# Recurrent mixer: block-diagonal matrices kept as 64 columns, products on the halves of the array

## The chip, the cores and the metric

The kernel runs on one core of a Trainium2 chip. TensorE multiplies, VectorE, ScalarE and GpSimd do the elementwise work, SyncE issues most DMAs. The metric is the device time of one execution in microseconds; smaller is better. Before the change three runs took 2711.81, 2712.51 and 2715.53 us, median 2712.51.

## The reference

The whole kernel computes two transformer-like blocks on 256 tokens: two layers with windowed attention and retention, then a layer with a recurrent mixer beside a latent attention, a layer with two more attentions, and a mixture of experts. The change touches one piece, the recurrent mixer (RWKV-7), with 8 heads of 64 features:

```python
def step(state, inp):
    r_t, w_t, k_t, v_t, kk_t, b_t = inp
    sa = jnp.einsum('bhvk,bhk->bhv', state, -kk_t)
    state = (state * w_t[:, :, None, :] + sa[..., None] * b_t[:, :, None, :]
             + v_t[..., None] * k_t[:, :, None, :])
    return state, jnp.einsum('bhvk,bhk->bhv', state, r_t)

_, y = lax.scan(step, state0, xs)        # 256 steps
```

It is followed by a group norm, a bonus term and a gate. All of it is fp32.

## The kernel before

The 256 steps are done in four chunks of 64. Inside a chunk the recurrence becomes matrix algebra: products between the chunk's keys and removal vectors, masked to a triangle, the inverse of a unit triangular 64x64 matrix, and a few products with the state. Only the state passes from chunk to chunk. Two chunks lie on the 128 partitions at once (a token tile `tt` of 128), so such a matrix is stored as 128x128 with two 64x64 blocks on the diagonal and zeros elsewhere, four heads side by side in a tile of 128x512 (`X`, line 153). The helper `each` (line 165) multiplies four of them into one PSUM tile with four matmuls of 128 columns.

The heads come in two groups `g` of four. `blocks` (line 226) makes the 16x16 diagonal blocks of the triangular matrices of all heads: four sets of four products (L163), masked on VectorE (L243), reduced to 16 columns (L245), written to memory (L247) and read back in another layout (L249). `inverses` (line 254) inverts all the 16x16 blocks at once on VectorE (L266, L268), through memory again (L271, L274). `group` (line 305) is a generator that runs once for each group: it extends the inverse to 64x64 (x, xt, p1 and the products b1, b2, L336 to L359), makes the factors tmt, wz, abr and akr, and then loops over the two chunks of the token tile: u from wz, the state and tmt (L384, L385), the new state (L392, L393) and the output (L397 to L399).

Head pairs share 128 partitions (head 2j on the lower 64, head 2j+1 on the upper), so k, r and wz of a single head are kept in zero-padded tiles zk, zr, zw and contracted over all 128 rows. Values and u get the same treatment for the chunks: vz and uz have one tile for each chunk with zeros in the other half, set once by GpSimd (L302).

What sets the order: the two `group` generators and the latent attention `mla` are advanced in turn by `rounds` (line 1335), and the tile framework's scheduler then orders each engine's queue from what is recorded. On TensorE the `blocks` products stand between the last input projections (L518 to L520, in fp32r, three passes for a high and a low part), and the last chunks between the first matmuls of the output projection.

In the trace a line of the form `sm<-zk,a 128*128 128x128 f32` is a matmul into tile sm: 128 rows times 128 columns of weights, and the moving operand of 128 rows and 128 columns. Every fp32 matmul shows up as two instructions. The tiles bb, kd, kb and kn of the code appear as a, kn, em (their buffers' names), wz as zw, and b1, b2, p1 as b and p.

Of the kernel before, what the change touches and what calls it, by code (L numbers as in the profile page):

```python
# [44 lines left out]
def _const_parts():  # L45
    f = np.float32
    i128 = np.arange(P)
    out = {}
# [6 lines left out]
    t = np.arange(S)  # L55
# [37 lines left out]
    s_ = i128[:, None]  # L93
    t_ = i128[None, :]
# [4 lines left out]
    out["m16"] = (b16 & up).astype(f)
    out["m1"] = (b32 & ~b16 & up).astype(f)  # L100
    out["m2"] = (b64 & ~b32 & up).astype(f)
    out["minc"] = (b64 & (s_ <= t_)).astype(f)
    out["mlow"] = (b64 & (s_ > t_)).astype(f)
    out["mb16"] = b16.astype(f)
# [38 lines left out]
class Rwkv:  # L143
# [18 lines left out]
    def mm(self, o, l, r):  # L162
        self.nc.tensor.matmul(o, l, r, start=True, stop=True)  # L163

    def each(self, fn):
        ps = self.b.smps()
        for i in range(4):
            fn(ps[:, i * P:i * P + P], i)
        return ps.rearrange("p (h t) -> p h t", h=4)

    def decays(self):

# [52 lines left out]
    def blocks(self):  # L225

        nc, b, mp = self.nc, self.b, self.mp
        self.z = []
        for g in range(2):
            z = [self.X(f"z{n}{g}") for n in "krw"]  # L230
            for t in z:
                for par in range(2):
                    nc.gpsimd.memset(t[64 - 64 * par:P - 64 * par, par::2], 0.0)
            self.z.append(z)
        lc = b.mk(mp, [P, 16, 16], F32, "b20")
        for tt in range(2):
            ts = slice(tt * P, tt * P + P)
            for g in range(2):
                zk = self.z[g][0]
                self.padded(zk, self.kd, g, ts)  # L240
                ps = self.each(lambda o, i: self.mm(o, self.bb[:, 2 * g + i // 2, ts], zk[:, i]))
                t = b.t2k().rearrange("p (h t) -> p h t", h=4)
                nc.vector.tensor_tensor(t, ps, self.mask("m16"), op=OP.mult)  # L243
                s0 = 8 * tt + 4 * g
                nc.vector.tensor_reduce(lc[:, s0:s0 + 4], t.rearrange("p h (b j) -> p h j b", b=8), axis=AX.X, op=OP.add)  # L245
        d1 = b.mk(b.dp, [16, P, 16], F32, "d1")
        nc.sync.dma_start(out=d1.rearrange("h s j -> s h j"), in_=lc)  # L247
        self.nt = b.mk(mp, [P, 16, 16], F32, "x0")
        nc.sync.dma_start(out=self.nt, in_=d1.rearrange("h (b i) j -> (h b) i j", i=16))  # L249

    def mask(self, m):
        return self.b.c(m)[:, None, :].to_broadcast([P, 4, P])

    def inverses(self):

# [20 lines left out]
    def queries(self):  # L276
# [21 lines left out]
        self.vz = [[b.mk(self.mp, [P, S], F32, f"vz{c}{g}") for c in range(2)] for g in range(2)]  # L298
        for g in range(2):
            for c in range(2):  # L300
                for t in (self.uz[g][c], self.vz[g][c]):
                    nc.gpsimd.memset(t[64 - 64 * c:P - 64 * c], 0.0)  # L302

    def group(self, g, yt):

# [5 lines left out]
        uz, vz = self.uz[g], self.vz[g]  # L311
        sg_ = self.st[:, 2 * g:2 * g + 2]
        X = lambda tag: self.X(tag + str(g))
        mb = b.c("mb16").rearrange("p (b j) -> p b j", b=8)[:, None].to_broadcast([P, 4, 8, 16])
        pr = lambda i: 2 * g + i // 2
        f = lambda i: slice(64 * i, 64 * i + 64)
        oj = lambda ps, i: ps[64 * (i % 2):64 * (i % 2) + 64, (i // 2) * 64:(i // 2) * 64 + 64]
        for tt in range(2):
            ts = slice(tt * P, tt * P + P)
            self.padded(zk, kd, g, ts)  # L320
            self.padded(zr, r, g, ts)

            tk = {}
            for n, src in (("kkt", kd), ("bbt", bb), ("kbt", kb), ("v", v)):
                ps = b.smps()
                for i in range(2):
                    nc.tensor.transpose(ps[:, i * P:i * P + P], src[:, 2 * g + i, ts], b.c("ident"))
                if n == "v":
                    for c in range(2):
                        nc.scalar.copy(vz[c][64 * c:64 * c + 64], ps[64 * c:64 * c + 64, :S])  # L330
                else:
                    tk[n] = b.mk(mp, [P, S], F32, n + str(g))
                    nc.scalar.copy(tk[n], ps[:, :S])
            b1, b2, p1 = X("b1"), X("b2"), X("p1")
            ps = each(lambda o, i: mm(o, bb[:, pr(i), ts], zk[:, i]))
            TT(b1, ps, self.mask("m1"), op=OP.mult)  # L336
            TT(b2, ps, self.mask("m2"), op=OP.mult)

            x, xt = X("x"), X("xt")
            s0 = 8 * tt + 4 * g  # L340
            for m, dst in ((0, x), (1, xt)):
                nc.gpsimd.tensor_tensor(dst.rearrange("p h (b j) -> p h b j", b=8),
                                        self.xc[:, m, s0:s0 + 4, None, :].to_broadcast([P, 4, 8, 16]), mb, op=OP.mult)
            yield
            nc.scalar.copy(p1, each(lambda o, i: mm(o, b1[:, i], x[:, i])))
            yield
            q1 = each(lambda o, i: mm(o, xt[:, i], p1[:, i]))
            TT(x, x, q1, op=OP.subtract)
            yield
            q2 = each(lambda o, i: mm(o, p1[:, i], xt[:, i]))  # L350
            TT(xt, xt, q2, op=OP.subtract)
            yield
            nc.scalar.copy(p1, each(lambda o, i: mm(o, b2[:, i], x[:, i])))
            ml = X("b1")
            ps = each(lambda o, i: mm(o, zk[:, i], kb[:, pr(i), ts]))
            TT(ml, ps, self.mask("mlow"), op=OP.mult)
            yield
            q2 = each(lambda o, i: mm(o, p1[:, i], xt[:, i]))
            TT(xt, xt, q2, op=OP.subtract)  # L359
            abr, akr = X("abr"), X("akr")  # L360
            ps = each(lambda o, i: mm(o, bb[:, pr(i), ts], zr[:, i]))
            TT(abr, ps, self.mask("minc"), op=OP.mult)
            yield
            tmt = X("tmt")
            nc.scalar.activation(tmt, each(lambda o, i: mm(o, ml[:, i], xt[:, i])), AF.Copy, scale=-1.0)
            ps = b.smps()
            for i in range(4):
                par = i % 2
                mm(ps[64 * par:64 * par + 64, (i // 2) * P:(i // 2) * P + P], tk["kkt"][:, f(i)], xt[:, i])
            for par in range(2):  # L370
                rows = slice(64 * par, 64 * par + 64)
                nc.scalar.activation(wz[rows, par::2], ps[rows, :S].rearrange("p (j t) -> p j t", j=2), AF.Copy, scale=-1.0)
            yield
            ps = each(lambda o, i: mm(o, kb[:, pr(i), ts], zr[:, i]))
            TT(akr, ps, self.mask("minc"), op=OP.mult)
            yield

            for c in range(2):
# [1627 lines left out]
```

## Time and profile before

| What | Value |
|---|---|
| median of three runs | 2712.51 us |
| the profiled execution's own time | 2711.97 us |
| its span, first to last instruction | 2710.2 us |
| TensorE busy | 2657.4 us, 98% of the span |
| VectorE / ScalarE / GpSimd busy | 73% / 58% / 7% |
| mean granted TensorE clock | 0.993 |
| matmul instructions | 15024 |

The span is what the trace covers; the execution's own time is 1.8 us longer. The busy share is an average over stages that differ much: the mixer's part is the roughly 120 us from 1188 to 1309 us, and it is read by itself below. The granted clock is 1 when TensorE runs at 2.4 GHz and 0.5 at 1.2 GHz.

### The profile page before, as it was taken

How to read it: one execution, taken by the hardware profiler on the slowest of the kernel's cores; microseconds unless marked ns; L12 is line 12 of the kernel's file. 1: busy time of each engine (PE TensorE's matmuls, PEld its weight loads, DVE VectorE, ACT ScalarE, POOL GpSimd, SP SyncE). 2: the span in 40 equal slices, each digit the busy share in tenths (PEclk: the TensorE clock that was granted, in tenths of full speed). 3: DMA queues.
4: the chain of work that ended last, by engine and by line, in shares of the span. 5: the costliest groups of instructions: out<-in, count | busy, mean ns of one | idle time of the engine just before them, and what ended most of it. 6: DMA issues, size and time to landing. Idle time of an engine off the chain costs nothing.

```text
span 2710.2 us, 39506 instructions
## 1 busy us (share of the span) xinstructions
PE 2657.4 (98%) x15024; PEld 2201.5 (81%) x15024; DVE 1975.8 (73%) x2951; ACT 1567.9 (58%) x2364; POOL 197.2 (7%) x244
## 2 busy tenths in 40 slices
PE   7999999999999999999999999999999999999998
PEld 5866788888887899888899988888887787788776
DVE  5255577767765687675655568999988898888886
ACT  4244444144355666564454465877777777777775
POOL 1121200000113100312200100000000000000000
PEclk9999999999999999999999999999999999999999
DMA  7244223444542265530355455999899999998992
GB/s 289 73 167 149 74 101 131 153 140 162 181 133 78 95 209 176 168 125 6 109 183 193 166 182 192 359 356 370 329 355 350 357 333 361 347 358 332 364 349 91
DMA packets 113875, 585.94 MB, mean 216 GB/s; under 512 B 19536, under 2 KB 23136, under 8 KB 68752
## 3 DMA queue, kind: packets, MB, share of 16 engines
q1 hardware_dynamic: 111440, 576.19, 58.8%
q0 software_dynamic: 2240, 7.16, 1.1%
q8 instruction: 120, 1.97, 0.3%
q14 instruction: 75, 0.61, 0.1%
HBM read 581.82 MB, written 1.47 MB: 215 GB/s over the span
## 4 chain that ended last, share of the span: by engine, by line
PE 63%; DVE 2%; ACT 1%; DMA 1%; issue 1%; POOL 0%; DVEq 0%; POOLq 0%; ACTq 0%
PE mm L519 14%; PE mm L518 14%; PE mm L520 14%; PE dn L519 4%; PE dn L518 4%; PE dn L520 4%; PE sm L163 1%; PE sm L1785 1%; DVE wl L488 1%; PE sm L589 1%; PE sm L1735 1%; ACT wh L487 0%; PE sm L574 0%; PE sm L1223 0%; DMA wf<-w_in 0%
## 5 line engine op out<-in xcount | busy, mean ns | idle before, releaser
L488 DVE TENSOR_TENSOR wl<-wf,wh 128x1024 fp32r<-128x1024 f32 (+3 forms) x1178 | 1215.0, 1060 | 362.3 <-ACT wh L487 356.6
L487 ACT CAST wh<-wf 128x1024 fp32r<-128x1024 f32 (+3 forms) x1178 | 1044.1, 912 | 564.1 <-PE mm L519 282.5
L518 PE MATMUL mm<-ah,wh 128*128 128x256 f32 (+1 forms) x1768 | 569.6, 325 | 3.8 <-ACT wh L487 1.7
L520 PE MATMUL mm<-ah,wl 128*128 128x256 f32 (+1 forms) x1768 | 567.4, 322 | 0.9 <-DVE wl L488 0.7
L519 PE MATMUL mm<-al,wh 128*128 128x256 f32 (+1 forms) x1768 | 567.6, 322 | 0.0
L518 PEld LDWEIGHTS mm<-ah,wh 128*128 128x128 f32 x1768 | 330.2, 188 | 43.4 <-issue 7.8
L519 PE MATMUL mm<-wl,xh 128*128 128x512 f32 x896 | 357.7, 399 | 2.0 <-DVE wl L488 2.0
L519 PEld LDWEIGHTS mm<-al,wh 128*128 128x128 f32 x1768 | 332.3, 188 | 32.3 <-issue 5.5
L520 PEld LDWEIGHTS mm<-ah,wl 128*128 128x128 f32 x1768 | 333.2, 189 | 30.8 <-issue 2.3
L518 PE MATMUL mm<-wh,xh 128*128 128x512 f32 x896 | 355.2, 396 | 0.0
L520 PE MATMUL mm<-wh,xl 128*128 128x512 f32 x896 | 353.4, 395 | 0.0
L519 PEld LDWEIGHTS mm<-wl,xh 128*128 128x128 f32 x896 | 168.2, 188 | 52.2 <-DVE wl L488 13.1
L518 PEld LDWEIGHTS mm<-wh,xh 128*128 128x128 f32 x896 | 168.3, 188 | 39.4 <-ACT xh L1737 0.2
L520 PEld LDWEIGHTS mm<-wh,xl 128*128 128x128 f32 x896 | 168.2, 188 | 37.3
L520 PE MATMUL dn<-wh,eal 128*128 128x512 f32 x448 | 180.6, 403 | 0.0
L519 PE MATMUL dn<-wl,eah 128*128 128x512 f32 x448 | 177.8, 397 | 0.0
L518 PE MATMUL mm<-gh,wh 128*128 128x256 f32 (+1 forms) x528 | 168.6, 319 | 0.0
L520 PE MATMUL mm<-gh,wl 128*128 128x256 f32 (+1 forms) x528 | 168.0, 318 | 0.0
L519 PE MATMUL mm<-gl,wh 128*128 128x256 f32 (+1 forms) x528 | 168.0, 318 | 0.0
L518 PE MATMUL dn<-wh,eah 128*128 128x512 f32 x448 | 157.7, 396 | 0.0
L520 PEld LDWEIGHTS mm<-gh,wl 128*128 128x128 f32 x528 | 99.9, 189 | 7.9
L519 PEld LDWEIGHTS mm<-gl,wh 128*128 128x128 f32 x528 | 99.9, 189 | 7.7
(514 smaller groups left out, 3426.9 us busy)
## 6 DMA issues: line engine op xcount, KB each, us to landing
wf<-moe_wg SPq DMA_DIRECT2D x112, 1024.0 KB, 6.9
wf<-moe_wu SPq DMA_DIRECT2D x112, 1024.0 KB, 6.8
wf<-moe_wd SPq DMA_DIRECT2D x112, 1024.0 KB, 6.4
wf<-w_mod SPq DMA_DIRECT2D x64, 768.0 KB, 4.4
wf<-w_up SPq DMA_DIRECT2D x88, 512.0 KB, 3.5
wf<-w_down SPq DMA_DIRECT2D x32, 704.0 KB, 4.0
wf<-w_out SPq DMA_DIRECT2D x32, 512.0 KB, 3.5
wf<-w_qkg SPq DMA_DIRECT2D x30, 512.0 KB, 4.6
```

The source lines that it names most:

```text
L163: self.nc.tensor.matmul(o, l, r, start=True, stop=True)
L487: nc.scalar.copy(dh, src)
L488: nc.vector.tensor_tensor(dl, src, dh.bitcast(F32), op=OP.subtract)
L518: nc.tensor.matmul(out, lh, rh, start=first, stop=False)
L519: nc.tensor.matmul(out, lh, rl, start=False, stop=False)
L520: nc.tensor.matmul(out, ll, rh, start=False, stop=last)
L589: self.nc.tensor.matmul(ps[:w.shape[1], :S], w, self.com[:, :S], start=True, stop=True)
L1735: nc.tensor.matmul(ps[:, m * S:m * S + S], src[:, tt, k * P:k * P + P], G[:, tt, e0:e0 + 2], start=tt == 0, stop=tt == 1)
L1785: nc.tensor.transpose(ps[:, j * P:j * P + P], s[:, j * P:j * P + P], self.c("ident"))
```

## The change

`X` tiles get 64 columns for each head instead of 128: partition s holds only its own block's columns. The masks are cut the same way (`own`), so masking, copying and subtracting work on 128x256 instead of 128x512 elements. `each` now makes eight matmuls of 64 columns: for each head one for the lower and one for the upper 64 tokens, which go to the lower and the upper 64 partitions of PSUM. Products of two compact tiles (`blocks`, the new local function) contract over 64 rows: they use 64 rows and 64 columns of the array, the lower or the upper half of each. Products with a zero-padded operand (zk, zr, wz) still contract over 128 rows, now with 64 columns of weights. In the chunk loop the products with u and v read just the 64 rows of their chunk, so v needs no padding: the vz tiles and the memsets go. wz is made for each chunk by itself.

The heart of the diff (the mask constants, reshapes with b=4 for b=8, and the shapes of the x and xt products change in the same way and are left out):

```diff
     def X(self, tag):
-        return self.b.mk(self.mp, [P, 4, P], F32, tag)
+        return self.b.mk(self.mp, [P, 4, 64], F32, tag)
...
     def each(self, fn):
         ps = self.b.smps()
         for i in range(4):
-            fn(ps[:, i * P:i * P + P], i)
-        return ps.rearrange("p (h t) -> p h t", h=4)
+            for c in range(2):
+                self.mm(ps[64 * c:64 * c + 64, 64 * i:64 * i + 64], *fn(i, slice(64 * c, 64 * c + 64)))
+        return ps[:, :S].rearrange("p (h t) -> p h t", h=4)
...
-                ps = self.each(lambda o, i: self.mm(o, self.bb[:, 2 * g + i // 2, ts], zk[:, i]))
+                ps = self.each(lambda i, cs: (self.bb[:, 2 * g + i // 2, ts][:, cs], zk[:, i, cs]))
...
+        blocks = lambda l, r: each(lambda i, cs: (l[cs, i], r[cs, i]))
+            of = lambda t: lambda i, cs: t[:, pr(i), ts][:, cs]
...
-            nc.scalar.copy(p1, each(lambda o, i: mm(o, b1[:, i], x[:, i])))
+            nc.scalar.copy(p1, blocks(b1, x))
...
-            ps = each(lambda o, i: mm(o, zk[:, i], kb[:, pr(i), ts]))
+            ps = each(lambda i, cs: (zk[:, i, cs], of(kb)(i, cs)))
...
-            ps = b.smps()
-            for i in range(4):
-                par = i % 2
-                mm(ps[64 * par:64 * par + 64, (i // 2) * P:(i // 2) * P + P], tk["kkt"][:, f(i)], xt[:, i])
+            for c, ps in enumerate((b.smps(), b.smps())):
+                cs = slice(64 * c, 64 * c + 64)
+                for i in range(4):
+                    mm(oj(ps, i), tk["kkt"][cs, f(i)], xt[cs, i])
...
-                    nc.tensor.matmul(up[cs, f(i)], tmt[:, i, cs], vz[c][:, f(i)], start=ch == 0, stop=True)
+                    nc.tensor.matmul(up[cs, f(i)], tmt[cs, i], vt[cs, f(i)], start=ch == 0, stop=True)
...
-                        nc.tensor.matmul(oj(sp, i), tk["bbt"][:, f(i)], u[:, f(i)], start=True, stop=False)
-                        nc.tensor.matmul(oj(sp, i), tk["kbt"][:, f(i)], vz[c][:, f(i)], start=False, stop=True)
+                        nc.tensor.matmul(oj(sp, i), tk["bbt"][cs, f(i)], u[cs, f(i)], start=True, stop=False)
+                        nc.tensor.matmul(oj(sp, i), tk["kbt"][cs, f(i)], vt[cs, f(i)], start=False, stop=True)
...
-                    nc.tensor.matmul(oj(yp, i), u[:, f(i)], abr[:, i, cs], start=ch == 0, stop=False)
-                    nc.tensor.matmul(oj(yp, i), vz[c][:, f(i)], akr[:, i, cs], start=False, stop=True)
+                    nc.tensor.matmul(oj(yp, i), u[cs, f(i)], abr[cs, i], start=ch == 0, stop=False)
+                    nc.tensor.matmul(oj(yp, i), vt[cs, f(i)], akr[cs, i], start=False, stop=True)
```

Line numbers after the change are one to three lower from line 334 on: L163 becomes L165, L384 and L385 become L383 and L384, L397 to L399 become L396 to L398, L518 to L520 become L517 to L519.

In TensorE's queue the first set of `blocks` stands like this before (sm is the set's PSUM tile, zk and a its operands, the mm rows are an input projection):

```order
L520 MATMUL mm_10803<-ah_10081,wl_10796 128x256
L163 MATMUL sm_10751<-zk_1961_10730,a_10462 128x128
L518 MATMUL mm_10803<-ah_10081,wh_10795 128x256
L163 MATMUL sm_10751<-zk_1961_10730,a_10462 128x128
L519 MATMUL mm_10803<-al_10082,wh_10795 128x256
L163 MATMUL sm_10751<-zk_1961_10730,a_10462 128x128
L520 MATMUL mm_10803<-ah_10081,wl_10796 128x256
L163 MATMUL sm_10751<-zk_1961_10730,a_10462 128x128
L518 MATMUL mm_10803<-ah_10081,wh_10799 128x256
L519 MATMUL mm_10803<-al_10082,wh_10799 128x256
```

and like this after:

```order
L519 MATMUL mm_10819<-ah_10081,wl_10812 128x256
L165 MATMUL sm_10751<-zk_1961_10730,a_10462 64x64
L517 MATMUL mm_10819<-ah_10081,wh_10811 128x256
L165 MATMUL sm_10751<-zk_1961_10730,a_10462 64x64
L518 MATMUL mm_10819<-al_10082,wh_10811 128x256
L165 MATMUL sm_10751<-zk_1961_10730,a_10462 64x64
L519 MATMUL mm_10819<-ah_10081,wl_10812 128x256
L165 MATMUL sm_10751<-zk_1961_10730,a_10462 64x64
L517 MATMUL mm_10819<-ah_10081,wh_10815 128x256
L165 MATMUL sm_10751<-zk_1961_10730,a_10462 64x64
L518 MATMUL mm_10819<-al_10082,wh_10815 128x256
L165 MATMUL sm_10751<-zk_1961_10730,a_10462 64x64
```

Four rows of 128x128 become eight of 64x64, and they still alternate one by one with the projection's full-width rows, so twice as many of those stand between the first and the last product of the set.

In the middle of the first group phase, TensorE's queue before (x, b, p and xt are compact matrices, em, zk and zr operands over all 128 rows; rows of both groups alternate):

```order
L163 MATMUL sm_11253<-x_2039_11091,b_2036_11082 128x128 x4
L163 MATMUL sm_11260<-em_10465,zk_1961_10730 128x128 x4
L163 MATMUL sm_11282<-x_2064_11165,b_2061_11156 128x128 x4
L163 MATMUL sm_11289<-em_10465,zk_1964_10739 128x128 x4
L163 MATMUL sm_11295<-xt_2040_11092,p_2037_11083 128x128 x4
L163 MATMUL sm_11303<-zr_1962_10731,a_10462 128x128 x4
```

and after:

```order
L165 MATMUL sm_11289<-x_2036_11099,b_2033_11086 64x64 x8
L165 MATMUL sm_11300<-em_10465,zk_1961_10730 64x64 x8
L165 MATMUL sm_11326<-x_2062_11177,b_2059_11164 64x64 x8
L165 MATMUL sm_11337<-em_10465,zk_1964_10739 64x64 x8
L165 MATMUL sm_11347<-xt_2037_11100,p_2034_11087 64x64 x8
L165 MATMUL sm_11359<-zr_1962_10731,a_10462 64x64 x8
```

The order of the sets stays, with eight small products for four. What the rows can't show: the sets of b and x and of xt and p now contract over 64 rows, those of em with zk and of zr with a over 128.

VectorE's queue behind the third and fourth set of `blocks`, before (L243 masks, L245 reduces, L488 splits weights, L282 is a product of the next step, `queries`):

```order
L243 TENSOR_TENSOR t2k_10776<-sm_10771,cB_1864_10233 128x512
L243 TENSOR_TENSOR t2k_10786<-sm_10781,cB_1864_10233 128x512
L245 TENSOR_REDUCE b_1967_10748<-t2k_10776 128x64
L245 TENSOR_REDUCE b_1967_10748<-t2k_10786 128x64
L488 TENSOR_TENSOR wl_10946<-wf_10943,wh_10945 128x512
L488 TENSOR_TENSOR wl_10950<-wf_10943,wh_10949 128x512
L1294 SCALAR_TENSOR_TENSOR v_10237<-mm_10840,V_61,v_10237 128x255
L282 TENSOR_TENSOR cum_10463<-r_10235,k_10236 128x1024
```

and after:

```order
L247 TENSOR_TENSOR t2k_10788<-sm_10779,cB_1864_10233 128x256
L487 TENSOR_TENSOR wl_10890<-wf_10883,wh_10889 128x512
L249 TENSOR_REDUCE b_1967_10748<-t2k_10788 128x64
L487 TENSOR_TENSOR wl_10962<-wf_10959,wh_10961 128x512
L247 TENSOR_TENSOR t2k_10802<-sm_10793,cB_1864_10233 128x256
L286 TENSOR_TENSOR cum_10463<-r_10235,k_10236 128x1024
L249 TENSOR_REDUCE b_1967_10748<-t2k_10802 128x64
```

The mask of the last set is no longer directly ahead of its reduction: the 128x1024 product of `queries` (now L286) has moved between them.

## Rows read from the trace of the kernel before

**Rows 1.** The page: engines' busy time, and the last chain by engine.

```profile
PE 2657.4 (98%) x15024; PEld 2201.5 (81%) x15024; DVE 1975.8 (73%) x2951; ACT 1567.9 (58%) x2364; POOL 197.2 (7%) x244
...
PE 63%; DVE 2%; ACT 1%; DMA 1%; issue 1%; POOL 0%; DVEq 0%; POOLq 0%; ACTq 0%
```

**Rows 2.** Table by stretches: length, then busy us of each engine (instructions).

```profile
1187.90:1204.80 16.90, 16.90 (x146) 16.90 (x145) 14.68 (x21) 7.81 (x16) 5.73 (x12) 1.00 0.56 153
1204.80:1218.70 13.90, 10.81 (x62) 8.80 (x60) 12.00 (x46) 8.10 (x22) 2.92 (x6) 0.88 0.27 100
1218.70:1309.10 90.40, 88.84 (x912) 75.63 (x912) 46.88 (x118) 40.30 (x113) 14.85 (x20) 1.00 0.04 8
```

**Rows 3.** The same table for line 163 alone, the third stage.

```profile
1218.70:1309.10 90.40, 40.29 (x336) 37.57 (x336) 1.00 0.04 8
```

**Rows 4.** Waits of TensorE in the third stage: total us, times, longest.

```profile
PE sm L1239 <- DVE t2k L1235: 1.3, 1, 1.3
```

**Rows 5.** Timeline, TensorE, full products: start us, duration us, then the instructions.

```profile
1240.32 1.06 PE L163 MATMUL sm<-zr,a 128*128 128x128 f32 x8
1241.21 1.06 PE L163 MATMUL sm<-xt,b 128*128 128x128 f32 x8
```

**Rows 6.** Timeline, TensorE, narrow products that alternate column halves.

```profile
1250.07 0.33 PE L398 MATMUL sm<-abr,uz 128*64 128x64 f32 x4
...
1250.30 0.34 PE L398 MATMUL sm<-abr,uz 128*64 128x64 f32 x4
```

**Rows 7.** Timeline, TensorE, narrow products on one column half.

```profile
1252.78 0.28 PE L385 MATMUL sm<-vz,tmt 128*64 128x64 f32 x2
1252.90 0.28 PE L384 MATMUL sm<-st,zw 128*64 128x64 f32 x2
```

**Rows 8.** Timeline, TensorE, from narrow to full and back.

```profile
1305.03 0.22 PE L398 MATMUL sm<-abr,uz 128*64 128x64 f32 x1
1305.18 0.39 PE L519 MATMUL mm<-al,wh 128*128 128x256 f32 x1
1305.41 0.28 PE L520 MATMUL mm<-ah,wl 128*128 128x256 f32 x1
1305.62 0.27 PE L399 MATMUL sm<-akr,vz 128*64 128x64 f32 x1
...
1305.72 0.22 PE L399 MATMUL sm<-akr,vz 128*64 128x64 f32 x1
```

**Rows 9.** Timeline, TensorE, `blocks` between the projections.

```profile
1187.57 0.28 PE L518 MATMUL mm<-ah,wh 128*128 128x256 f32 x1
1187.69 0.28 PE L519 MATMUL mm<-al,wh 128*128 128x256 f32 x1
...
1187.93 0.38 PE L163 MATMUL sm<-zk,a 128*128 128x128 f32 x2
...
1188.28 0.38 PE L163 MATMUL sm<-zk,a 128*128 128x128 f32 x2
...
1193.66 0.38 PE L163 MATMUL sm<-zk,a 128*128 128x128 f32 x2
```

**Rows 10.** Chain of waits across the inverses: start us, us, what.

```profile
1198.34 3.83 DMA d<-b
...
1205.01 0.24 DVE xt L266
...
1217.49 0.39 DVE b L269
...
1223.10 1.40 POOL x L342 x2
```

**Rows 11.** Groups by line on VectorE, 1187.5 to 1219 us.

```profile
L245 DVE TENSOR_REDUCE b<-t2k 128x64 f32<-128x512 f32 x4 | 4.1, 1034 | 0.0
...
L282 DVE TENSOR_TENSOR cum<-r,k 128x1024 f32<-128x1024 f32 x1 | 1.2, 1214 | 0.0
...
L1331 DVE TENSOR_TENSOR t2k<-mm,cB 128x256 f32<-128x256 f32 x1 | 0.4, 417 | 0.0
```

More of the change, by code (lines that the diff above doesn't have):

```diff
@@ L98, in _const_parts @@
     up = s_ < t_
[L99 to L104, printed above, removed]
+    own = lambda m: np.where(s_ < 64, m[:, :64], m[:, 64:]).astype(f)
+    out["m16"] = own(b16 & up)
+    out["m1"] = own(b32 & ~b16 & up)
+    out["m2"] = own(b64 & ~b32 & up)
+    out["minc"] = own(b64 & (s_ <= t_))
+    out["mlow"] = own(b64 & (s_ > t_))
+    out["mb16"] = own(b16)
     out["seg"] = np.tile((np.arange(S) % 64 != 0).astype(f), (P, 1))
@@ L229, in blocks @@
         for g in range(2):
-            z = [self.X(f"z{n}{g}") for n in "krw"]
+            z = [self.b.mk(mp, [P, 4, P], F32, f"z{n}{g}") for n in "krw"]
             for t in z:
@@ L240, in blocks @@
                 self.padded(zk, self.kd, g, ts)
-                ps = self.each(lambda o, i: self.mm(o, self.bb[:, 2 * g + i // 2, ts], zk[:, i]))
-                t = b.t2k().rearrange("p (h t) -> p h t", h=4)
+                ps = self.each(lambda i, cs: (self.bb[:, 2 * g + i // 2, ts][:, cs], zk[:, i, cs]))
+                t = b.t2k()[:, :S].rearrange("p (h t) -> p h t", h=4)
                 nc.vector.tensor_tensor(t, ps, self.mask("m16"), op=OP.mult)
                 s0 = 8 * tt + 4 * g
-                nc.vector.tensor_reduce(lc[:, s0:s0 + 4], t.rearrange("p h (b j) -> p h j b", b=8), axis=AX.X, op=OP.add)
+                nc.vector.tensor_reduce(lc[:, s0:s0 + 4], t.rearrange("p h (b j) -> p h j b", b=4), axis=AX.X, op=OP.add)
         d1 = b.mk(b.dp, [16, P, 16], F32, "d1")
@@ L251, in mask @@
     def mask(self, m):
-        return self.b.c(m)[:, None, :].to_broadcast([P, 4, P])
+        return self.b.c(m)[:, None, :].to_broadcast([P, 4, 64])
     def inverses(self):
@@ L297, in queries @@
         self.uz = [[b.mk(self.mp, [P, S], F32, f"uz{c}{g}") for c in range(2)] for g in range(2)]
[L298 to L302, printed above, removed]
     def group(self, g, yt):
@@ L310, in group @@
         zk, zr, wz = self.z[g]
-        uz, vz = self.uz[g], self.vz[g]
+        uz = self.uz[g]
         sg_ = self.st[:, 2 * g:2 * g + 2]
         X = lambda tag: self.X(tag + str(g))
-        mb = b.c("mb16").rearrange("p (b j) -> p b j", b=8)[:, None].to_broadcast([P, 4, 8, 16])
+        mb = b.c("mb16").rearrange("p (b j) -> p b j", b=4)[:, None].to_broadcast([P, 4, 4, 16])
         pr = lambda i: 2 * g + i // 2
@@ L327, in group @@
                     nc.tensor.transpose(ps[:, i * P:i * P + P], src[:, 2 * g + i, ts], b.c("ident"))
[L328 to L333, printed above, removed]
+                tk[n] = b.mk(mp, [P, S], F32, n + str(g))
+                nc.scalar.copy(tk[n], ps[:, :S])
+            vt = tk["v"]
             b1, b2, p1 = X("b1"), X("b2"), X("p1")
-            ps = each(lambda o, i: mm(o, bb[:, pr(i), ts], zk[:, i]))
+            ps = each(lambda i, cs: (of(bb)(i, cs), zk[:, i, cs]))
             TT(b1, ps, self.mask("m1"), op=OP.mult)
@@ L341, in group @@
             for m, dst in ((0, x), (1, xt)):
-                nc.gpsimd.tensor_tensor(dst.rearrange("p h (b j) -> p h b j", b=8),
-                                        self.xc[:, m, s0:s0 + 4, None, :].to_broadcast([P, 4, 8, 16]), mb, op=OP.mult)
+                nc.gpsimd.tensor_tensor(dst.rearrange("p h (b j) -> p h b j", b=4),
+                                        self.xc[:, m, s0:s0 + 4, None, :].to_broadcast([P, 4, 4, 16]), mb, op=OP.mult)
             yield
-            nc.scalar.copy(p1, each(lambda o, i: mm(o, b1[:, i], x[:, i])))
+            nc.scalar.copy(p1, blocks(b1, x))
             yield
-            q1 = each(lambda o, i: mm(o, xt[:, i], p1[:, i]))
+            q1 = blocks(xt, p1)
             TT(x, x, q1, op=OP.subtract)
             yield
-            q2 = each(lambda o, i: mm(o, p1[:, i], xt[:, i]))
+            q2 = blocks(p1, xt)
             TT(xt, xt, q2, op=OP.subtract)
             yield
-            nc.scalar.copy(p1, each(lambda o, i: mm(o, b2[:, i], x[:, i])))
+            nc.scalar.copy(p1, blocks(b2, x))
             ml = X("b1")
-            ps = each(lambda o, i: mm(o, zk[:, i], kb[:, pr(i), ts]))
+            ps = each(lambda i, cs: (zk[:, i, cs], of(kb)(i, cs)))
             TT(ml, ps, self.mask("mlow"), op=OP.mult)
             yield
-            q2 = each(lambda o, i: mm(o, p1[:, i], xt[:, i]))
+            q2 = blocks(p1, xt)
             TT(xt, xt, q2, op=OP.subtract)
             abr, akr = X("abr"), X("akr")
-            ps = each(lambda o, i: mm(o, bb[:, pr(i), ts], zr[:, i]))
+            ps = each(lambda i, cs: (of(bb)(i, cs), zr[:, i, cs]))
             TT(abr, ps, self.mask("minc"), op=OP.mult)
@@ L364, in group @@
             tmt = X("tmt")
-            nc.scalar.activation(tmt, each(lambda o, i: mm(o, ml[:, i], xt[:, i])), AF.Copy, scale=-1.0)
-            ps = b.smps()
-            for i in range(4):
-                par = i % 2
-                mm(ps[64 * par:64 * par + 64, (i // 2) * P:(i // 2) * P + P], tk["kkt"][:, f(i)], xt[:, i])
-            for par in range(2):
-                rows = slice(64 * par, 64 * par + 64)
-                nc.scalar.activation(wz[rows, par::2], ps[rows, :S].rearrange("p (j t) -> p j t", j=2), AF.Copy, scale=-1.0)
+            nc.scalar.activation(tmt, blocks(ml, xt), AF.Copy, scale=-1.0)
+            for c, ps in enumerate((b.smps(), b.smps())):
+                cs = slice(64 * c, 64 * c + 64)
+                for i in range(4):
+                    mm(oj(ps, i), tk["kkt"][cs, f(i)], xt[cs, i])
+                for par in range(2):
+                    rows = slice(64 * par, 64 * par + 64)
+                    nc.scalar.activation(wz[rows, par::2, cs], ps[rows, :P].rearrange("p (j t) -> p j t", j=2), AF.Copy, scale=-1.0)
             yield
-            ps = each(lambda o, i: mm(o, kb[:, pr(i), ts], zr[:, i]))
+            ps = each(lambda i, cs: (of(kb)(i, cs), zr[:, i, cs]))
             TT(akr, ps, self.mask("minc"), op=OP.mult)
```

## The prediction

> **What bounds the kernel now.** I read the page first: TensorE is busy 2657.4 of 2710.2 us and the chain of work that ended last is 63% TensorE matmuls [rows 1]. The change touches only the recurrent mixer, so the next view is the table by stretches, cut where the mixer's phases change [rows 2]. From 1187.9 to 1204.8 us the four sets of products of `blocks` are interleaved with the last input projections, and TensorE is busy 16.90 of 16.90 us. From 1204.8 to 1218.7 it is busy 10.81 of 13.90 us: this stage waits for the small triangular inverses. From 1218.7 to 1309.1 run both `group` generators and the attention between them: 88.84 of 90.40 us busy at a granted clock of 1.00. The view of waits shows how little TensorE waits there: its longest wait is 1.3 us [rows 4]. So in the first and third stage TensorE's own time is the time, and the halved evictions on VectorE, ScalarE and GpSimd can return at most those 1.6 idle us. In the second stage the chain of waits counts [rows 10]: a DMA that starts at 1198.34, the inverses on VectorE from 1205.01 to 1217.88, and two more DMAs until GpSimd builds x at 1223.10. That is 24.8 us which the change leaves alone, except that GpSimd's tiles halve.
>
> **What a product costs in each shape.** Line 163 takes 40.29 us of the third stage [rows 3]. A `matmul` in fp32 shows up as two instructions. A set of four full products (128x128 weights, 128 columns) starts at 1240.32, the next at 1241.21: 0.89 us a set [rows 5]. With 64 weight columns and 64 moving columns a product on one half of the array takes 0.117 us (1252.78 to 1252.90) [rows 7]. When consecutive products alternate between the two column halves they overlap: four products, eight instructions, in 0.23 us (1250.07 to 1250.30), which is 0.058 us each [rows 6]. So a set of eight small products takes 0.47 us if the halves overlap and 0.94 us if they do not. The unchanged 0.89 us lies between the two, nearly at the slower one.
>
> The third price is that of changing the width. At 1305.03 a 64-wide product starts, and the full one behind it at 1305.18 instead of 0.06 us later: 0.09 us lost. The next full one comes 0.23 us on, where 0.12 is the pace (1187.57 to 1187.69 [rows 9]): 0.11 lost. The way back loses 0.09 us (1305.41 to 1305.62) and then 0.05 (1305.62 to 1305.72 instead of 0.058) [rows 8]. Going to the full array costs 0.20 us, to the narrow one 0.14, a round trip 0.34.
>
> **Part 1, `blocks`.** Before, full fp32 products alternate with full fp32r products at 0.34 us a pair (1187.93 to 1188.28), which is 0.22 + 0.12: the alternation is free, because both use the whole array [rows 9]. After the change the order of TensorE's queue has 32 narrow products up to the end of the fourth set, and 36 full ones between them, with 27 round trips. That is 36 x 0.12 + 32 x 0.117 + 27 x 0.34 = 4.3 + 3.7 + 9.2 = 17.2 us from 1187.93, so the fourth set ends near 1205.1; before, its last product starts at 1193.66. VectorE then has the mask (0.42 us at 128x256, as L1331), a 1.21 us product (L282) that the new order puts ahead of the last reduction, and that reduction (half of 1.03) [rows 11]: 2.2 us, so the DMA starts near 1207.3 instead of 1198.34. That is 9 us later. GpSimd's first two tiles, half as long (1.40 us for two in the chain [rows 10]), return 0.6. I take +8 us at the start of the groups. Bounds: 0, if the alternation is free as it was before (the fourth set then ends near 1196, and VectorE, which lagged 4 us behind it, ends where it did), and +9. TensorE's own queue agrees: the stage grows by 9 us, and the 13.9 us behind it, of which 3.1 are idle, cannot hide more than those.
>
> **Part 2, the groups.** From the queue's order between L1439/L1440 and the last chunk: 38 sets fall from 0.89 to 0.47 us, -16.0 us. The four kkt products per set are now eight on quarters of the array, about -0.8. Changes between full and 64 columns go from 47 to 49, +0.3. New are 113 changes between products with 128 rows (the zero-padded zk, zr and wz are still contracted over 128) and products with 64 rows. No row shows one, since every matmul before has 128 rows. Nearest is the change to 64 columns at 0.14 us; 0 and 0.20 are the ends. At 0.14 they cost +15.8 us. 90 of them are inside the chunk loop, where L383 and L384 now alternate, as do L396 and the pair L397, L398. In the three later y blocks of each group the overlap of column halves goes too, since each head changes rows before the other half follows: 24 instructions took 0.70 us at the overlapped pace and take 1.40 alone, six times, +4.2. Sum -16.0 - 0.8 + 0.3 + 15.8 + 4.2 = +3.5; with some idle time at the joints I take +4.
>
> A rule speaks for this price. The Trainium skill, "TensorEngine Tiling (Array Packing)", Key Properties, says that changing the tiling mode, not just the tile, drains the engine. The 0.09 us gaps of [rows 8] agree for the width; that it holds for rows no row here shows. By the rule the sum stands; without it the 15.8 and the 4.2 go.
>
> **Part 3, the rest.** Eight memsets on GpSimd vanish, four copies of v replace eight on ScalarE, eight wz evictions become sixteen shorter ones: all beside TensorE's 88.84 busy us, so nothing, and at worst the 1.6 idle us grow by as much again.
>
> **Sum.** The profiled execution took 2711.97 us, 0.5 under the median of the three, 2712.51. 2711.97 + 8 + 4 = 2724 us. Later stages are bound by TensorE and would carry a shift through.
>
> **Rivals.**
> - *The change of rows is free.* For it: the 128-row and the 64-row product on one column half use the same columns, and only width changes are seen to cost. Against: the array is re-partitioned in both cases. It is one mechanism and lands on the other side of zero: the loop's 20.0 us vanish and the sets' 16.8 stay, so 2711.97 + 8 - 16.5 = 2703.5 us. It decides as soon as a row change costs under about 0.05 us (then 16.5 - 5.7 - half of 4.2 outweighs the 8).
> - *The two row halves do not overlap.* Both halves of a set write one PSUM tile, and the trace has no row halves. The 24 sets between compact tiles then take 0.94 instead of 0.47 us: +11.3, 2735 us. With the chunk loop's s and y products held up too it is more. A page has this as a rule: the Trainium skill, "TensorEngine Tiling (Array Packing)", Gotcha 1, says that different row tiles cannot access the same PSUM bank at once; no row here shows whether that holds when the partitions differ.
> - *The delay of `blocks` is absorbed.* The inverses' chain has VectorE work of other parts between its steps (12.9 us for 31 short instructions), which could move ahead of the wait; then only the 4 of the groups remain: 2716 us. Against: the DMAs before it are serial and their start is what moves.
>
> **How the numbers follow.** Forecast 0.54, free row changes 0.22, no overlap of row halves 0.12, absorbed delay 0.12. About 0.2% (5.4 us) is what a measurement can tell from no change, so "same" is 2707 to 2718. Faster 0.21: nearly all of the first rival. Same 0.18: the absorbed delay and the low end of the forecast, where a row change costs 0.08 or less. Slower 0.61: the rest of the forecast, and the missing overlap. The forecast's own range, a row change between 0.08 and 0.20 us and +5 to +9 for `blocks`, is 2714 to 2732. The range to hold 8 in 10 reaches into the rivals: 2701 (both gains: free rows and a part of the 8 hidden) to 2738 (no overlap).
>
> **What would show it.** Right: L165 in the narrow products of `blocks` with gaps of about 0.15 and 0.21 us around each full product, the DMA d<-b starting near 1207, and the stretch of the groups near 94 us. In the chunk loop L383 to L384 would start about 0.2 us after each other instead of 0.06. Wrong: L383 and L384 at the old pace (first rival); sets L165 between compact tiles at 0.94 us (second); x by GpSimd before 1228 (third). A drop of the granted clock below 1.00 inside the groups would add time that none of these terms holds: it was 1.00 over the whole stage before, narrow products included [rows 2].

## The result, and the profile after

The changed kernel takes 2742.8 us (median of 4 runs, 2739.8 to 2751.0), beside 2712.8 us of four runs of the kernel before: a ratio of 1.0114, 95% interval 1.0101 to 1.0128. The medians are 30 us apart, where 12 were forecast, and the time lies above the range's upper end of 2738. The profiled execution has a span of 2738.0 us at a mean granted clock of 0.985; before it was 2710.2 us at 0.993. Of the experiments' executions one, at 3062 us and a granted clock of 0.803, was disturbed and stands in none of the times below.

The table by stretches, cut where the same phases begin, has the columns of [rows 2]; the number behind the instruction counts is the granted clock. First the kernel before, its third stage cut once more: at GpSimd's first x, at the first chunk loop and at its end.

```profile
1222.90:1248.40 25.50, 25.34 (x204) 22.03 (x200) 14.42 (x33) 11.95 (x30) 12.61 (x15) 1.00 0.04 5
1248.40:1309.10 60.70, 59.33 (x693) 51.01 (x692) 29.58 (x81) 26.79 (x80) 2.23 (x5) 1.00 0.01 2
```

The changed kernel: `blocks`, the wait for the inverses, the first sets, and the chunk loops (with the second half's sets between them).

```profile
1187.90:1212.20 24.30, 24.30 (x166) 19.57 (x166) 10.66 (x18) 7.85 (x16) 6.95 (x13) 1.00 0.35 96
1212.20:1232.30 20.10, 17.40 (x98) 11.83 (x97) 13.54 (x50) 8.26 (x20) 1.58 (x4) 0.75 0.28 79
1232.30:1252.90 20.60, 18.37 (x362) 14.77 (x357) 10.85 (x31) 11.10 (x34) 8.38 (x15) 1.00 0.06 7
1252.90:1340.80 87.90, 85.78 (x870) 65.10 (x868) 27.01 (x82) 25.72 (x83) 1.98 (x5) 0.77 0.01 3
```

GpSimd's timeline has its first x 9.5 us later than the 1223.10 of [rows 10]: the forecast's +8.

```profile
1232.56 1.41 POOL L340 TENSOR_TENSOR x<-xc,cB 128x256 f32<-128x256 f32 x2 [13.74 <-DMA xc<-d]
```

The first sets fall from 25.5 to 20.6 us. The chunk loops grow from 60.7 to 87.9 us, and there the column of the granted clock reads 0.77 instead of 1.00. A clock of 0.77 over 87.9 us is 0.23 x 87.9 = 20.2 us lost; without it the loops would have taken 67.7. That sum takes everything in the slow stretches as doubled, and so it is an upper estimate: row changes slow down less (0.14 to 0.19 us, below), 48 of them stand in the slow stretches of this trace, and 48 x 0.045 makes the loss nearer 18. The sums below go by the 20.2. So of +31.7 us at the end of the groups (1340.8 against 1309.1) 9.4 stand ahead of them, -4.9 in the sets, +7.0 in the loops at full clock, and +20.2 are the clock. At the program's end 27.8 of the 31.7 are left. Forecast were +8, then +4 for sets and loops together, and for the clock nothing.

The same stretch in slices of 8 us shows that the clock goes between its two levels, 2.4 and 1.2 GHz, and that TensorE is fully busy at the lower one:

```profile
1248.00:1256.00 8.00, 7.36 (x152) 6.06 (x150) 4.04 (x15) 5.42 (x20) 1.84 (x3) 1.00 0.01 2
1256.00:1264.00 8.00, 8.00 (x58) 5.48 (x57) 0.29 (x1) 1.11 (x3) 0.00 (x0) 0.57 0.01 2
1264.00:1272.00 8.00, 8.00 (x61) 6.14 (x61) 2.43 (x9) 1.62 (x6) 1.19 (x3) 0.71 0.00 0
1272.00:1280.00 8.00, 8.00 (x50) 6.07 (x49) 1.01 (x3) 1.47 (x5) 0.80 (x2) 0.50 0.01 2
1280.00:1288.00 8.00, 8.00 (x51) 5.17 (x51) 3.27 (x8) 3.08 (x10) 0.00 (x0) 0.72 0.00 0
1288.00:1296.00 8.00, 6.48 (x130) 5.20 (x126) 3.94 (x12) 3.71 (x13) 0.00 (x0) 1.00 0.01 2
...
1304.00:1312.00 8.00, 8.00 (x131) 6.20 (x127) 3.76 (x12) 4.92 (x17) 0.00 (x0) 1.00 0.01 2
...
1320.00:1328.00 8.00, 8.00 (x36) 5.88 (x37) 0.58 (x2) 1.49 (x4) 0.00 (x0) 0.50 0.00 0
```

Read the instruction counts beside the busy time: 36 to 61 instructions fill 8.00 us in the slow slices, 130 to 152 stand in those at 1.00, sets among them. The busy column alone hides both the slower clock and the gaps: in the rows below a product's duration reaches past the start of the next one even where the two are 0.26 or 0.40 us apart. TensorE's waits say the same. In the whole of the two last stretches the longest is this one (total us, times, longest us),

```profile
PE sm L1238 <- DVE t2k L1234: 2.8, 3, 1.5
```

where it was 1.3 before [rows 4]. TensorE's idle time in these two stretches went from 1.5 to 4.4 us, so waits took some 3 us and not the 22.

The timeline of the chunk loop in the changed kernel, first at half clock, then at full clock (start us, duration us, then the instructions; L383 contracts over 128 rows, L384 over 64):

```profile
1257.52 0.42 PE L398 MATMUL sm<-akr,v 64*64 64x64 f32 x2
1257.87 0.47 PE L383 MATMUL sm<-st,zw 128*64 128x64 f32 x2
...
1258.68 0.47 PE L383 MATMUL sm<-st,zw 128*64 128x64 f32 x2
1259.08 0.47 PE L384 MATMUL sm<-v,tmt 64*64 64x64 f32 x2
1259.48 0.47 PE L383 MATMUL sm<-st,zw 128*64 128x64 f32 x2
...
1264.10 0.33 PE L383 MATMUL sm<-st,zw 128*64 128x64 f32 x2
1264.36 0.33 PE L384 MATMUL sm<-v,tmt 64*64 64x64 f32 x2
1264.61 0.33 PE L383 MATMUL sm<-st,zw 128*64 128x64 f32 x2
...
1267.04 0.28 PE L398 MATMUL sm<-akr,v 64*64 64x64 f32 x2
...
1269.76 0.31 PE L397 MATMUL sm<-abr,uz 64*64 64x64 f32 x1
1269.86 0.42 PE L398 MATMUL sm<-akr,v 64*64 64x64 f32 x2
1270.21 2.07 PE L1452 MATMUL mm<-ql,wuqr 128*128 128x256 f32 x4
```

At full clock a product follows the other after 0.26 us, where 0.117 is its pace without a change of rows [rows 7]: 0.14 a change, the forecast's value. At half clock it is 0.40, against 0.21 for two instructions at that clock's pace (0.10 from 1269.76 to 1269.86): 0.19. The last row shows who pays as well: the attention's full products between the loops run at half clock too, four instructions in 2.07 us. Before they took half of that:

```profile
1220.54 1.03 PE L1453 MATMUL mm<-ql,wuqr 128*128 128x256 f32 x4
```

### The profile page after: what moved, and what is told of

It reads as the page before. It is cut to its first block, busy times and chain, and to the rows that moved or that the text cites. A ratio compares the mean times of both kernels' runs of the same rounds, so it can differ in the third digit from the quotient of the medians.

```text
span 2738.0 us, 40265 instructions
## 1 busy us (share of the span) xinstructions
PE 2682.3 (98%) x15408; PEld 2206.7 (81%) x15408; DVE 1964.9 (72%) x2951; ACT 1565.5 (57%) x2368; POOL 191.4 (7%) x236
## 4 chain that ended last, share of the span: by engine, by line
PE 63%; DVE 2%; ACT 1%; issue 1%; DMA 1%; POOL 0%; DVEq 0%; ACTq 0%; POOLq 0%; SPq 0%
PE mm L518 14%; PE mm L517 14%; PE mm L519 14%; PE dn L518 4%; PE dn L517 4%; PE dn L519 4%; PE sm L165 1%; PE sm L1784 1%; PE sm L588 1%; DVE wl L487 1%; PE sm L1734 1%; ACT wh L486 0%; PE sm L1222 0%; PE sm L397 0%; PE sm L384 0%
## 5 line engine op out<-in xcount | busy, mean ns | idle before, releaser
L517 PE MATMUL mm<-ah,wh 128*128 128x256 f32 (+1 forms) x1768 | 569.7, 326 | 3.9 <-ACT wh L486 1.7
L519 PE MATMUL mm<-ah,wl 128*128 128x256 f32 (+1 forms) x1768 | 567.0, 322 | 1.0 <-DVE wl L487 0.7
L518 PE MATMUL mm<-al,wh 128*128 128x256 f32 (+1 forms) x1768 | 567.4, 322 | 0.0
L517 PEld LDWEIGHTS mm<-ah,wh 128*128 128x128 f32 x1768 | 331.3, 188 | 45.0 <-issue 7.8
L518 PE MATMUL mm<-wl,xh 128*128 128x512 f32 x896 | 357.9, 399 | 2.0 <-DVE wl L487 2.0
L518 PEld LDWEIGHTS mm<-al,wh 128*128 128x128 f32 x1768 | 333.1, 188 | 32.8 <-issue 5.5
L519 PEld LDWEIGHTS mm<-ah,wl 128*128 128x128 f32 x1768 | 332.7, 188 | 31.7 <-issue 2.5
L517 PE MATMUL mm<-wh,xh 128*128 128x512 f32 x896 | 354.6, 396 | 0.0
L519 PE MATMUL mm<-wh,xl 128*128 128x512 f32 x896 | 353.7, 395 | 0.0
L518 PEld LDWEIGHTS mm<-wl,xh 128*128 128x128 f32 x896 | 168.2, 188 | 52.4 <-DVE wl L487 13.1
L517 PEld LDWEIGHTS mm<-wh,xh 128*128 128x128 f32 x896 | 168.3, 188 | 39.4 <-ACT xh L1736 0.2
L519 PEld LDWEIGHTS mm<-wh,xl 128*128 128x128 f32 x896 | 168.3, 188 | 37.0
L519 PE MATMUL dn<-wh,eal 128*128 128x512 f32 x448 | 180.6, 403 | 0.0
L518 PE MATMUL dn<-wl,eah 128*128 128x512 f32 x448 | 177.7, 397 | 0.0
L517 PE MATMUL mm<-gh,wh 128*128 128x256 f32 (+1 forms) x528 | 168.6, 319 | 0.0
L519 PE MATMUL mm<-gh,wl 128*128 128x256 f32 (+1 forms) x528 | 168.0, 318 | 0.0
L518 PE MATMUL mm<-gl,wh 128*128 128x256 f32 (+1 forms) x528 | 168.0, 318 | 0.0
L517 PE MATMUL dn<-wh,eah 128*128 128x512 f32 x448 | 157.7, 396 | 0.0
L519 PEld LDWEIGHTS mm<-gh,wl 128*128 128x128 f32 x528 | 99.9, 189 | 7.9
L518 PEld LDWEIGHTS mm<-gl,wh 128*128 128x128 f32 x528 | 99.9, 189 | 7.7
```

Source lines behind the costliest of these rows:

```text
L517: nc.tensor.matmul(out, lh, rh, start=first, stop=False)
L518: nc.tensor.matmul(out, lh, rl, start=False, stop=False)
L519: nc.tensor.matmul(out, ll, rh, start=False, stop=last)
```

## The experiments

Theory A: a change of rows empties the array for 0.14 us, and the chunk loops, which have little else in them, let the granted clock fall to 1.2 GHz. Theory B: quarter-array products do that by themselves, in any order. Theory C: the clock falls because the stage before starts later and waits longer. "Row changes" counts, in the order of TensorE's queue over the whole program, the neighbours of which one has 128 rows and the other 64: 142 in the changed kernel, none before. Ratios are against the kernel before on the same chip: 2713.0 us (median of 23) for the first four experiments, 2713.7 (of 13) for the others. In the code, `nc.tensor.` and most start and stop arguments are left out, and ... stands for further lines of the same kind.

**Chunk loop back at 128 rows.** The tiles stay compact; v and u get their zero halves back.

```
- matmul(up[cs, f(i)], tmt[cs, i], vt[cs, f(i)])
+ matmul(up[cs, f(i)], tmt[:, i], vz[c][:, f(i)])
- matmul(oj(yp, i), u[cs, f(i)], abr[cs, i])
+ matmul(oj(yp, i), u[:, f(i)], abr[:, i])
...
```

> The changed kernel with the chunk loop alone put back to 128 rows (v and u padded with zeros as before); the sets and `blocks` stay compact. Row changes in TensorE's queue fall from 142 to 34 in the whole program. Theory A (each row change empties the array for 0.14 us, and these gaps let the granted clock fall to 1.2 GHz in the chunk loops, which costs some 20 us more): 108 x 0.14 = 15, 4 for the overlap and 20 for the clock come back, near 2743 - 39 = 2704 us, granted clock 1.00 in the loops. Theory B (64-row products lower the clock by themselves, whatever their order): the loops have none left, so 2704 too, but a clock below 1.00 among the compact sets. Theory C (the clock falls because the stage before starts later and has longer gaps): the clock still falls, 2724.

Measured: 2711.2 us, ratio 0.999 (0.9978 to 1.0003), so the whole loss of 30 us is gone. Its chunk loops, in the same columns:

```profile
1255.90:1310.90 55.00, 52.32 (x879) 42.91 (x875) 26.04 (x82) 26.37 (x85) 2.24 (x5) 1.00 0.01 3
```

The clock stays at 1.00, which speaks against theory C, since `blocks` was still late here; but the stage before read 1.00 here too, not 0.75, so that theory is decided only with the full `blocks` below. The loops take 55.0 us: 87.9 - 55.0 = 32.9, of which 20.2 are the clock and 12.7 the row changes and the lost overlap. For these two 15 + 4 were expected, and the 6 us missing there are most of the 7 by which 2704 was missed. Some 2 of them come from the upper estimate of the clock: it counts a change at half clock (0.19) as 0.095 at full clock, where it is 0.14. Single runs spread from 2702.6 to 2718.5.

**Same products, grouped.**

```
+ if ch:
+     for i in range(4):
+         mm(up[cs, f(i + 4)], wz[:, i, cs], sg_[:, i // 2])
  for i in range(4):
-     if ch:
-         matmul(up[cs, f(i)], wz[:, i, cs], sg_[:, i // 2], start=True, stop=False)
-     matmul(up[cs, f(i)], tmt[cs, i], vt[cs, f(i)], start=ch == 0, stop=True)
+     mm(up[cs, f(i)], tmt[cs, i], vt[cs, f(i)])
...
+ if ch:
+     TT(u[cs], u[cs], up[cs, S:], op=OP.add)
```

> The changed kernel with the chunk loop's 64-row products as they are, but in each block all products over 128 rows stand ahead of all those over 64 rows, into columns of their own in the same PSUM tile, and VectorE adds the two parts. Row changes fall from 142 to 66; the number of products of each shape is the same. Theory A: 76 x 0.14 = 11 come back and the clock drops little or not, 20: 2712 to 2720 us, less what VectorE's two additions in the chain cost (some 5 us at most). Theory B: the clock falls as it did, 2730 us. Theory C: as B.

Measured: 2718.2 us, ratio 1.0024 (1.0009 to 1.0038).

```profile
1254.00:1312.30 58.30, 55.73 (x870) 44.55 (x868) 29.85 (x93) 25.29 (x83) 2.02 (x5) 1.00 0.01 2
```

The loops have as many TensorE instructions as the changed kernel's (870), of the same shapes, and the clock stays at 1.00. That rules out theory B: it is the order, not the quarter-array product. Its timeline shows one change where four pairs stood:

```profile
1258.68 0.68 PE L165 MATMUL sm<-st,zw 128*64 128x64 f32 x8
1259.29 0.68 PE L165 MATMUL sm<-v,tmt 64*64 64x64 f32 x8
```

Four products and the change behind them take 0.61 us, eight 1.2. Alternating, eight take 4 x 0.51 = 2.0 at full clock (1264.10 to 1264.61) and 4 x 0.80 = 3.2 at half.

**`blocks` back at full products.**

```
- ps = self.each(lambda i, cs: (self.bb[...][:, cs], zk[:, i, cs]))
+ ps = b.smps()
+ for i in range(4):
+     self.mm(ps[:, i * P:i * P + P], self.bb[:, 2 * g + i // 2, ts], zk[:, i])
...
```

> The changed kernel with the four sets of `blocks` alone put back to full products (128x128, mask and reduction too). Theories A and B: the 9.5 us by which the groups started later come back, the chunk loops stay as they are: 2733 us, with the clock still near 0.5 in the loops. Theory C: the clock stays up, 2712.

Measured: 2733.4 us, ratio 1.008 (1.0065 to 1.0096), 9.4 us under the changed kernel. GpSimd's x starts where it did before, and the clock falls all the same. The DMA behind `blocks`, x, and the loops:

```profile
1195.63 3.72 DMA d<-b
```

```profile
1223.40 1.40 POOL L342 TENSOR_TENSOR x<-xc,cB 128x256 f32<-128x256 f32 x2 [12.89 <-DMA xc<-d]
```

```profile
1242.80:1327.90 85.10, 82.98 (x869) 63.46 (x868) 27.02 (x82) 25.70 (x83) 1.99 (x5) 0.80 0.01 3
```

So theory C falls, Part 1 of the forecast is confirmed in size, and the delay is carried to the end rather than absorbed.

**The chunk loop's row changes alone, in the kernel before.**

```
- matmul(up[cs, f(i)], tmt[:, i, cs], vz[c][:, f(i)])
+ matmul(up[cs, f(i)], tmt[cs, i, cs], vt[cs, f(i)])
...
```

> The kernel before with the chunk loop's products on v and u alone made 64 rows long; sets and `blocks` stay full. 108 row changes where there were none. Theory A: 15 + 4 + 20 on top of 2712.8, near 2752 us, and the clock falls to 1.2 GHz in the loops. Theory B: the same. Theory C: the clock stays at 1.00 and the prices alone count, 2732 us.

Measured: 2744.3 us (median of six), ratio 1.0107 (1.0089 to 1.0126), so 29 us slower than before. The trace is that of a second group of runs:

> The kernel before with the chunk loop alone at 64 rows once more, for its trace (that of the first time was disturbed). Theory A: near 2742 us as timed, L-for-L the sets at 0.89 us and `blocks` as before, and the granted clock at 0.5 in parts of the chunk loops. Rival (the 29 us are row changes alone, at 0.27 us each): clock 1.00 throughout and gaps of 0.27 us.

Measured: 2742.5 us (two runs), ratio 1.0104 (1.0087 to 1.0122), with sets and `blocks` as before. The loops, and a slice of them:

```profile
1251.50:1339.70 88.20, 86.86 (x693) 70.00 (x692) 30.41 (x81) 26.51 (x78) 1.99 (x5) 0.85 0.01 2
...
1320.00:1328.00 8.00, 8.00 (x35) 5.88 (x34) 0.42 (x1) 1.22 (x3) 0.00 (x0) 0.50 0.00 0
```

The edit of the loop's row count alone makes the kernel nearly as slow as the whole change does. The loops grow by 27.5 us, 13.2 of them clock (0.15 x 88.2) and 14.3 at full clock, against the 15 and 4 expected. The rival, by which the 29 us are dearer row changes at full clock, falls.

**Fewer changes in the loop.** Every second head has its own products first.

```
+ ops = own + both if i % 2 else both + own
```

> The changed kernel with every second head's products in the reverse order (64-row ones ahead of the 128-row one), so that two heads in a row share a mode. Row changes fall from 142 to 102, nothing else changes. Theory A: 40 x 0.14 = 5.6 come back; of the 20 us that the clock costs some part, since the gaps are fewer: between 2717 (clock at 1.00) and 2737 us (clock as in the changed kernel). Theory B (64-row products by themselves): 2737.

Measured: 2726.9 us, ratio 1.0053 (1.0037 to 1.0069), between the two bounds of theory A and well under the 2737 of theory B.

```profile
1256.50:1325.00 68.50, 66.38 (x869) 51.76 (x866) 26.89 (x82) 25.45 (x83) 1.97 (x5) 0.90 0.01 2
```

At full clock the loops take 61.6 us, 6.1 less than the changed kernel's 67.7: 40 changes at 0.15. The clock still costs 6.9. Side by side:

| kernel | row changes | loops, us | clock | lost to it, us |
|---|---|---|---|---|
| before | 0 | 60.7 | 1.00 | 0 |
| loop at 128 rows | 34 | 55.0 | 1.00 | 0 |
| grouped | 66 | 58.3 | 1.00 | 0 |
| every second head reversed | 102 | 68.5 | 0.90 | 6.9 |
| before, loop at 64 rows | 108 | 88.2 | 0.85 | 13.2 |
| full `blocks` | 142 | 85.1 | 0.80 | 17.0 |
| changed | 142 | 87.9 | 0.77 | 20.2 |

Each row is one execution. The mean clock of the whole program, which every run has, keeps this order: its median is 0.9835 in the changed kernel, 0.985 with full `blocks`, 0.988 with the loop alone at 64 rows, 0.989 with every second head reversed, 0.990 grouped, and 0.993 with the loop at 128 rows and before. The grouped kernel's twelve runs spread from 0.986 to 0.993, so its loss of 0 is that of one run.

**Compact sets only.** Both parts undone, loop and `blocks`; what is left of the change are the 64-column tiles and half-array sets of the groups.

> The chunk loop back at 128 rows and `blocks` back at full products; only the sets of the groups and their tiles stay compact. Theory A (row changes at 0.14 us, the clock that they pull down, and the width changes in `blocks`): the two undone parts add up, 2742.8 - 31.6 - 9.4 = 2702 us, some 11 under the kernel before, granted clock 1.00 from the first set to the last chunk. Rival (the two overlap: groups that start earlier only wait elsewhere): 2711, as with the loop alone.

Measured: 2705.8 us, ratio 0.9968 (0.9953 to 0.9982). The ratios of the two runs with one part undone add up to 0.9956, which lies in this interval, so within the noise the two parts add up. This version beats both kernels, the one before by 8 to 9 us.

```profile
1227.40:1249.00 21.60, 19.37 (x367) 15.62 (x367) 11.95 (x34) 10.83 (x35) 8.57 (x15) 1.00 0.05 6
1249.00:1304.00 55.00, 52.32 (x880) 42.91 (x875) 26.04 (x82) 26.38 (x85) 2.23 (x5) 1.00 0.01 2
```

Sets and loops together take 76.6 us where the kernel before needs 86.2.

**Padded sets on their head's own rows too.**

```
- ps = each(lambda i, cs: (of(kb)(i, cs), zr[:, i, cs]))
+ mm(ps[cs, 64 * j:64 * j + 64], kb[rs, pj + j, ts][:, cs], r[rs, pj + j, ts][:, cs])
...
```

> As the loop at 128 rows and the full `blocks` together, and the 20 sets that were contracted over 128 rows with zeros (zk, zr) now run over the 64 rows of their own head, one PSUM tile for each half of the rows, so that all four quarters of the array can work at a time. If they do, such a set falls from 0.47 to 0.23 us: 20 x 0.24 = 5 less, 2697 us. If the quarters run two at a time: no change, 2702. VectorE gets 24 more short evictions, in the chain of a group at three places of each half: up to 4 us more.

Measured: 2703.1 us, ratio 0.9963 (0.9948 to 0.9977), which its interval doesn't tell from the one above. The sets do get quicker, 0.41 us for sixteen instructions and the change of rows behind them:

```profile
1246.43 0.47 PE L165 MATMUL sm<-r,em 64*64 64x64 f32 x16
1246.84 0.33 PE L401 MATMUL sm<-vz,tmt 128*64 128x64 f32 x2
```

but the first sets and the loops read a clock of 0.92 and 0.97 where both were 1.00:

```profile
1225.50:1246.80 21.30, 18.77 (x354) 14.41 (x350) 11.06 (x36) 10.66 (x33) 7.04 (x11) 0.92 0.05 6
1246.80:1303.00 56.20, 53.39 (x876) 42.72 (x868) 26.24 (x93) 26.09 (x85) 2.23 (x5) 0.97 0.01 2
```

Its trace has 36 row changes, the version above 34, so more changes are not the reason here.

## Why the prediction was wrong

**Direction and Part 1 right.** `blocks` between the projections alternates widths at the forecast's price: a pair of narrow and full product starts every 0.57 us, where 0.12 + 0.117 + 0.34 = 0.58 was worked out.

```profile
1185.71 0.33 PE L165 MATMUL sm<-zk,a 128*64 128x64 f32 x2
...
1188.01 0.33 PE L165 MATMUL sm<-zk,a 128*64 128x64 f32 x2
1188.27 0.38 PE L518 MATMUL mm<-al,wh 128*128 128x256 f32 x1
1188.58 0.33 PE L165 MATMUL sm<-zk,a 128*64 128x64 f32 x2
```

The four sets took 17.1 us (1185.71 to 1202.83), forecast 17.2. In this execution they began 2.2 us earlier than before, so the DMA named as a sign starts near 1205 and not at 1207, 6.6 us later than in [rows 10]. x is 9.5 us late all the same: from that DMA to x the changed kernel takes 27.6 us, where the prediction left 24.8 alone. With full `blocks` it is 27.8 (1195.63 to 1223.40), so the compact `blocks` are not the reason, and what is stays open. That +8 came out in this pair of traces is thus partly luck; the clean test is the run with full `blocks`, in which the DMA starts 9.3 us earlier and the median falls by 9.4.

```profile
1202.56 0.27 PE sm L165 x2
...
1204.97 3.86 DMA d<-b
```

**The sets right.** From x to the first chunk loop 4.9 us went, and a set of sixteen instructions takes 0.47 us: fourteen of them take 0.40 (1237.03 to 1237.43), and the 0.61 from 1237.43 to 1238.04 are a set and 0.14 for the change of shape behind it.

```profile
1237.03 0.57 PE L165 MATMUL sm<-p,xt 64*64 64x64 f32 x14
1237.43 0.63 PE L165 MATMUL sm<-xt,p 64*64 64x64 f32 x16
1238.04 0.46 PE L1221 MATMUL sm<-e,sg 128*128 128x128 f32 x2
```

That disposes of the rival of row halves that don't overlap, although both halves write one PSUM tile. The Trainium skill, "TensorEngine Tiling (Array Packing)", Gotcha 1, would have them wait for each other; here, on different partitions of one PSUM tile, they don't.

**The row change right, its company forgotten.** The 0.14 us is what the trace shows, so the rival of free row changes fell. At full clock the groups changed by -4.9 + 7.0 = +2.1 us (some +4 by the lower estimate of the clock's loss), forecast +3.5 to +4. There is luck in that: up to the last chunk the forecast counted 113 row changes, 90 of them in the loop, and the queue has 142, of which 108 go with the loop. The missing 29 at 0.14 would have made it 4 us more; which other term gave them back is not shown.

**The step that failed** is the one that took the groups' durations at the clock of 1.00 "over the whole stage before, narrow products included" [rows 2], and kept that clock for a stage into which it put 113 gaps. The prediction named a lower clock as the thing that none of its terms holds, and gave it neither a term nor a chance. It was the largest term: 20.2 of the 31.7 us. The forecast with it would have been 2724 + 20 = 2744; that this is so near to 2742.8 is luck too, since 4 of the 31.7 us at the end of the groups were gone at the program's end. The narrow products of [rows 6, 7] ran back to back at full clock, which is what a row before could show and no more; grouped 64-row products do the same. The Trainium skill, "TensorE: Matmul & The Clock Gate", Part 1, has the rule that bears on it: the throttled clock is the default, and activity releases it. The runs of the table agree in direction: none with 66 row changes or fewer lost anything in its loops, and from 102 to 142 the loss rises from 6.9 to 20.2 us.

What stays open is what starts a fall. In the changed kernel the clock had fallen before 1257.52, where a pair of L398 takes 0.42 us instead of 0.28, and the first block that alternates starts behind that, at 1257.87; the first chunk's blocks hold few row changes. In the grouped kernel the same first-chunk products passed at 1.00. Short falls also came with few row changes or none, behind a wait of TensorE. The first two rows are from the version with the padded sets on 64 rows, the two behind them from the kernel before with the loop alone at 64 rows, among its first sets, ahead of any row change:

```profile
1236.77 0.39 PE L1255 MATMUL sm<-ccom,t2k 128*128 128x128 f32 x1 [1.87 <-DVE t2k L1251]
1237.38 1.06 PE L1239 MATMUL sm<-e,sg 128*128 128x256 f32 x2
```

```profile
1226.31 2.81 PE L163 MATMUL sm<-x,b 128*128 128x128 f32 x16 [2.24 <-POOL x L334]
1228.91 1.92 PE L163 MATMUL sm<-p,xt 128*128 128x128 f32 x8
```

The number in brackets is the wait, 1.87 and 2.24 us; the eight instructions of the last row take 1.92 us, where [rows 5] has 1.06. In the version with compact sets only, a wait of 1.5 us left the clock at 1.00. So the order of the products, and with it the number of row changes, is shown as the cause of most of the loss (grouping alone takes it from 20.2 us to 0, alternating alone from 0 to 13.2), not as the only thing that lowers the clock; a single block is shown as neither. Nor do the runs say where between 66 and 102 changes the loss begins.

## What to carry to other kernels

Before small products are cut further, count in the queue's order how often neighbouring ones differ in rows or columns of the array: here each change cost at least as much as the small product itself (0.14 us beside 0.117). Where TensorE is the bound, a forecast needs a row of its own for the granted clock: here the stage that got emptier paid for its gaps and then for everything else in it, other work's products too, at half speed. Group the products that use the same rows and columns, or keep one shape throughout: half-size products paid where they ran in unbroken sets of eight, and cost time where a product of another shape stood between one and the next.

## What had not been expected of the hardware

- A change between 128 and 64 rows costs 0.14 us at 2.4 GHz and 0.19 us at 1.2 GHz, so it doesn't double with the clock as the products do (0.117 to 0.21).
- All four quarters of the array worked at a time in the sets whose row halves write different PSUM tiles: sixteen instructions and a row change in 0.41 us, some 0.27 without the change, where two quarters take 0.47.
- TensorE reads as busy for 8.00 of 8.00 us in a slice in which it issues 36 instructions and in one in which it issues 131: the granted clock and the counts tell them apart, the busy share doesn't.
